# A hybrid convolution and attention layer on one Trainium2 core: first products taken slice by slice, prompt attention in fixed rows, a shorter norm at the end

## The chip, the cores and the metric

The kernel runs on one core of one Trainium2 chip. The metric is the device time of one execution in microseconds (us), as the median of several. The engines of the core are TensorE (PE; its weight loads are listed as PEld), VectorE (DVE), ScalarE (ACT), GpSimd (POOL) and SyncE (SP), which here only issues DMAs. Each engine works through its own instructions in order, and semaphores tie the engines together. Matmul results go to PSUM, everything else lies in SBUF.

## The reference

One layer of a decoder for 256 prompt tokens and 8 x 4 sample tokens, which share the weights. All 288 tokens go through each product together.

```python
z = x @ w_in                                   # h, gate_b, gate_c, q, k, v, g_a, g_b
ya = gate_b * causal_conv3(gate_c * h)          # mixer A
yb = dilated_window_attention(q, k, v)          # mixer B: 3 groups x 4 heads of 128, ALiBi;
                                                # the softmax of a head runs over its 3 groups
mixed = sigmoid(g_a) * (ya @ w_branch_a) + sigmoid(g_b) * (yb @ w_branch_b)
x1 = layernorm(ALPHA * x + mixed @ w_out)
a, b = split(x1 @ w_up)
y = layernorm(ALPHA * x1 + (silu(causal_conv3(a)) * b) @ w_down)
```

D_MODEL is 2048, D_FF 5632. The outputs are y, the new keys and values, and the rows that the convolutions keep. The sample tokens attend to caches of up to 2048 old rows, the prompt tokens to themselves.

## The kernel before

**Layout and products.** Activations are held feature by token: 128 partitions, 16 slices k, 288 tokens. A product is one block of 128 output features: `product` (L174) takes the next prepared weight block and `mms` (L188) issues, for each of its 16 slices, three matmuls of 288 columns: the rounded weight times the rounded activation (L194), the rounded weight times the activation's remainder (L195), the weight's remainder times the rounded activation (L196). So a block of 16 slices is 48 matmuls.

**Weights.** `prepare` (L161) loads one block of 1 MB into one of three buffers `wst`; `half_block` (L134) makes, for each half of it, the rounded part on ACT (`whi`, L137) and the remainder on VectorE (`wlo`, L138). One block is prepared ahead of its product in the program's text. A scheduler then places the instructions of each engine; the program can hold an order with `behind` (L124), which makes one instruction stand after another of its engine without a wait.

**The start.** L213 is a loop of matmuls on a zero tile, to busy TensorE early. Then x is loaded in four pieces (`FIRST`, L221, issued by ACT), and the first two blocks in the same four pieces each (L232, issued by SP). Rounded parts and remainders follow (L234, L235 for weights, `split`, L200 and L201, for x). The first product then runs over all its slices, and after it the second; the scheduler interleaves them where one has to wait.

**Order of the work.** The first 36 products are 12 query blocks, then four heads of six key and value blocks (their copies are at L435 and L445). Then come 48 products for mixer A, the gates, the branches, w_out, and the feed-forward part in three thirds. After a head's keys and values, `prompt_attention` (L271) is written out in full: the values are transposed (L276) and copied out of PSUM; for each half of the queries come three score matmuls (L283), the bias on VectorE (L285), maximum, exponential and scaling (L289 to L293), then for each half of the keys three transposes (L298), a copy (L300) and three value matmuls (L302). All of these use the two PSUM buffers `att`. The scheduler places these matmuls among the products that follow.

**Sample attention.** `sample_steps` (L342) is a generator; `product` takes a step of it from time to time. A step is a visit: 16 or 64 records of small matmuls with 32 rows of output on a cache tile (scores at L356, values at L407), into the PSUM buffer `long`, and the load of the next cache tiles.

**Norms.** `Norm` (L542 on) keeps sums on POOL, squares on ACT, and at the end multiplies by a matrix of ones on TensorE (L572, L573). The reciprocal root is made by Ln (L608 for the last norm), Exp (L609) and one Newton step (L616, L617). Ln and Exp lie in different activation tables, and the table of Ln is called early by a dummy activation (L568). `finish_out` (L593 on) splits the last pass among VectorE and POOL (subtract the mean and multiply by the factor, L604) and ACT and VectorE (gain and shift, L630 and L628), and stores y in six pieces (L631).

Of the kernel before, what the change touches and what calls it, by code (L numbers as in the profile page):

```python
# [17 lines left out]
P = 128  # L18
D = 2048
KD = D // P  # L20
# [45 lines left out]
FIRST = ((0, 2), (2, 6), (8, 4), (12, 4))  # L66

N_WARM = 20
# [14 lines left out]
def layer_kernel(ctx: ExitStack, tc: tile.TileContext, ins, outs):  # L83
# [89 lines left out]

    def product(x):  # L174
# [12 lines left out]

    def mms(out, w, x):  # L188
        nk = sum(n for _, _, n in w)
        k = 0  # L190
        for hi, lo, n in w:
            for c in range(n):
                xh_k, xl_k = (t[:, k].rearrange("p h a -> p a h") for t in x)
                pe.matmul(out, hi[:, c, :], xh_k, start=k == 0, stop=False)  # L194
                pe.matmul(out, hi[:, c, :], xl_k, start=False, stop=False)  # L195
                pe.matmul(out, lo[:, c, :], xh_k, start=False, stop=k == nk - 1)  # L196
                k += 1
# [22 lines left out]
    for k0, n in FIRST:  # L220
        act.dma_start(xs[:, k0 : k0 + n, :], x_in[:, k0 : k0 + n, :])  # L221
    w_ready = []
    stage = []
    for b in range(2):
        stage.append((sb(wp, [P, KD, P], "wst"), ins["w_in"][b].rearrange("p (k c) -> p k c", c=P)))
        halves = [[sb(wp, [P, HK, P], n, F32R, bufs=4) for n in ("whi", "wlo")] + [HK] for _ in range(2)]
        w_ready.append(halves)
    for k0, n in FIRST:
        k = slice(k0, k0 + n)
        h = slice(k0 % HK, k0 % HK + n)  # L230
        for b, (st, src) in enumerate(stage):
            sp.dma_start(st[:, k, :], src[:, k, :])  # L232
            hi, lo, _ = w_ready[b][k0 // HK]
            act.copy(hi[:, h, :], st[:, k, :])  # L234
            dve.tensor_tensor(lo[:, h, :], st[:, k, :], f32(hi[:, h, :]), ALU.subtract)  # L235
            if b == 0:
                split(xh[:, k, :, :H], xl[:, k, :, :H], h3(xs[:, k]))
    x = (xh[:, :, :, :H], xl[:, :, :, :H])
    x_gb = (xh[:, :, :, :HG], xl[:, :, :, :HG])

# [13 lines left out]
    sT_two = [xs_flat[:, c * NG * P : (c + 1) * NG * P].rearrange("p (g q) -> p g q", g=NG) for c in range(2)]  # L254
    oT_two = [xs_flat[:, c * P + 6 * P : c * P + 7 * P] for c in range(2)]
    q_all = xs_flat[:, 8 * P : 8 * P + NH * NG * T].rearrange("p (j g t) -> p j g t", j=NH, g=NG)
# [13 lines left out]

    def prompt_attention(j, qT, kT, vT):  # L271
        v = v_two[j % 2]
        for kb in range(2):
            pv = att(NG * P)
            for g in range(NG):
                pe.transpose(pv[:, g * P : (g + 1) * P], vT[:, g, kb * P : (kb + 1) * P], ident)  # L276
            act.copy(v[:, kb], pv.rearrange("p (g d) -> p g d", g=NG))
        for qb in range(2):
            nk = P * (qb + 1)
            s = s_two[qb][:, : NG * nk].rearrange("p (g k) -> p g k", g=NG)  # L280
            for g in range(NG):
                p = att(nk)
                pe.matmul(p, qT[:, g, qb * P : (qb + 1) * P], kT[:, g, :nk], start=True, stop=True)  # L283
                c0 = qb * NG * P + g * nk
                dve.scalar_tensor_tensor(  # L285
                    s[:, g, :], m_dist[:, c0 : c0 + nk], -SLOPE[g][j] / SCALE, p, ALU.mult, ALU.add
                )
            st = sb(wk, [P, 4], "st", bufs=4)
            dve.reduce_max(st[:, 0:1], s, AX.XY)  # L289
            dve.tensor_scalar_mul(st[:, 1:2], st[:, 0:1], -SCALE)  # L290
            act.activation(s, s, AF.Exp, bias=st[:, 1:2], scale=SCALE, accum_out=st[:, 2:3])
            dve.reciprocal(st[:, 3:4], st[:, 2:3])
            dve.tensor_scalar_mul(s, s, st[:, 3:4])  # L293
            po = att(P)
            for kb in range(qb + 1):
                pt = att(NG * P)
                for g in range(NG):
                    pe.transpose(pt[:, g * P : (g + 1) * P], s[:, g, kb * P : (kb + 1) * P], ident)  # L298
                sT = sT_two[kb]
                act.copy(sT, pt.rearrange("p (g q) -> p g q", g=NG))  # L300
                for g in range(NG):
                    pe.matmul(po, v[:, kb, g, :], sT[:, g, :], start=kb == 0 and g == 0, stop=kb == qb and g == NG - 1)  # L302
            oT = oT_two[qb]
            act.copy(oT, po)
            split(ybh[:, j, qb * P : (qb + 1) * P], ybl[:, j, qb * P : (qb + 1) * P], oT)
# [36 lines left out]
    def sample_steps():  # L342
        fetch_two()
        yield
        s = sw2[:, :SW]
        sbias = cst[:, C_SB : C_SB + SW]
        for g in range(NG):
            qm = by_batch(q_s[:, g])
            cols = P if g == 0 else NT * P
            p = sb(ps, [P, cols], "long", bufs=1)  # L350
            for b in range(NB):
                if g > 0 or b % 4 == 0:
                    c = cache_tiles.pop(0)
                o = (b % 4) * NH * P if g == 0 else 0
                for j in range(NH):
                    pe.matmul(  # L356
                        p[j * NS : (j + 1) * NS], qm[:, j, b, :], c[:, o + j * cols : o + (j + 1) * cols],
                        start=b == 0, stop=b == NB - 1,
                    )
                if b == NB - 1 or (g > 0 and b % 2 == 1):  # L360
                    fetch_two()
# [35 lines left out]
        for g in range(NG):  # L397
# [4 lines left out]
            for b in range(NB):  # L402
# [3 lines left out]
                for j in range(NH):  # L406
                    pe.matmul(  # L407
                        p[j * NS : (j + 1) * NS], sm[:, j, b, :], c[:, o + j * cols : o + (j + 1) * cols],
                        start=b == 0 and g < 2, stop=b == NB - 1 and g == 2,
                    )  # L410
                if b == NB - 1 or (g > 0 and b % 2 == 1):
                    fetch_two()
                    yield
# [18 lines left out]
    kv = sb(big, [P, 2, 2, NG, T], "dd")  # L432
    for j in range(NH):
        for g in range(NG):
            act.copy(h2(q_all[:, j, g]), product(x))  # L435
            if j == 0 and g > 0:
                for dst, src in ((cst, ins["cst"][:, :C_M0]), (m_dist, ins["cst"][:, C_M0:])) if g == 1 else ((prm, ins["prm"]),):
                    behind(sp.dma_start(dst, src), w_load[0])
        pool.tensor_copy(q_s[:, :, j, :], q_all[:, j, :, SEQ:])
    steps_on[0] = True  # L440
    for j in range(NH):
# [8 lines left out]
        prompt_attention(j, q_all[:, j], kT, vT)  # L450
# [43 lines left out]
    yah = sb(big, [P, KD, T], "yah", F32R)  # L494
    yal = sb(big, [P, KD, T], "yal", F32R)
    cm = sb(big, [P, KD, 2 + 2 * NB], "cm")
    for i in range(KD):
# [10 lines left out]
        pb = product(x)  # L508
        ya = sb(wk, [P, T], "ya", bufs=2)
# [32 lines left out]
    class Norm:  # L542
# [13 lines left out]
        def add(self, i):  # L556
# [9 lines left out]
            if i == KD - 2:  # L566

                act.activation(lw[:, 3, 0:1], q[:, 0:1], AF.Ln)  # L568
# [9 lines left out]
        def finish(self):  # L578
# [5 lines left out]
            act.activation(t, v, AF.Ln)  # L584
            act.activation(r, t, AF.Exp, scale=-0.5)
# [7 lines left out]
        def finish_out(self, y, out):  # L593
# [11 lines left out]

            for k0, n in MEAN_POOL:
                by_token(pool, k0, n, mu, ALU.subtract)
            act.activation(t, v, AF.Ln)  # L608
            act.activation(r, t, AF.Exp, scale=-0.5)  # L609
            with tc.issue_after(i_v.ins):  # L610
                for k0, n in MEAN_DVE:
                    i_m = by_token(dve, k0, n, mean, ALU.subtract)

            act.activation(t, r, AF.Square)
            with tc.issue_after(i_m.ins):
                dve.scalar_tensor_tensor(t, t, -0.5, v, ALU.mult, ALU.mult)  # L616
                i_r = dve.scalar_tensor_tensor(dev, t, 1.5, r, ALU.add, ALU.mult)  # L617
            act.copy(r_pool, dev)
            for k0, n in OUT_POOL:
                by_token(pool, k0, n, r_pool, ALU.mult)  # L620
            with tc.issue_after(i_r.ins):
                for k0, n in OUT_DVE:
                    i_m = by_token(dve, k0, n, dev, ALU.mult)
            for k0, n in OUT_ORDER:
                for i in range(k0, k0 + n):
                    if i in OUT_LAST:
                        with tc.issue_after(i_m.ins):
# [271 lines left out]
```

## Time and profile before

| | us |
|---|---|
| median of 3 runs | 1771.77 |
| lowest and highest of them | 1770.14 and 1772.48 |
| profiled execution | 1772.71 |
| its span, first to last instruction | 1770.9 |

| stretch of the profiled execution | from the span's start, us |
|---|---|
| first matmul on the zero tile | 1.22 |
| first product matmul | 5.41 |
| first and last record of prompt attention on TensorE | 119.25, 290.3 |
| first and last visit of sample attention | 146.49, 706.3 |
| last product matmul starts | 1752.47 |
| last output DMA issued, landed | 1766.26, 1769.93 |

A row of the timeline gives the start, the duration, the engine, the line, the operation, what is written and read, the shape and the count; a wait stands in brackets with what ended it. A float32 matmul of the attention shows as two records, a transpose or a product matmul as one. Matmuls overlap in their records, so the pace is read from the distance of their starts.

### The profile page before, as it was taken

Reading aid. Unit: us, or ns where it says so; the run is one execution under the profiler, and the core shown is the slowest. Engines: PE = TensorE matmul, PEld = TensorE weight load, DVE = VectorE, ACT = ScalarE, POOL = GpSimd, SP = SyncE. Lnnn points to the kernel's source line nnn. Section 1 sums busy time; section 2 is a strip of 40 time slices with the busy share of each in tenths; the row PEclk is TensorE's granted clock in tenths of the full one; section 3 lists DMA queues with packets and bytes.
Section 4 is the critical chain, followed back from the end, with each engine's and each line's share of the span. In section 5 each row is a group of like instructions: output and inputs, shape, how many; then the busy total and the mean of one; then the engine's idle time right before and its main releaser. Section 6 shows DMA issues by size and latency. Waiting matters only on the chain.

```text
span 1770.9 us, 33606 instructions
## 1 busy us (share of the span) xinstructions
PE 1749.3 (99%) x14277; PEld 1717.1 (97%) x14277; DVE 1010.0 (57%) x1321; ACT 800.8 (45%) x1178; POOL 252.4 (14%) x402
## 2 busy tenths in 40 slices
PE   8999999999999999999999999999999999999996
PEld 8999899999999999999999999999999999999996
DVE  4445446555645444455688787774555554555564
ACT  5444434333434333344455655553444443345444
POOL 0000000000000000001255233320011110011174
PEclk9999999999999999999999999999999999999998
DMA  8476677788787787467766566666666666666652
GB/s 305 172 301 258 258 292 272 288 304 316 260 322 301 296 322 264 151 247 270 283 218 235 214 226 226 226 226 223 229 227 226 230 222 233 219 236 219 242 191 104
DMA packets 59430, 436.25 MB, mean 246 GB/s; under 512 B 7184, under 2 KB 7696, under 8 KB 15248
## 3 DMA queue, kind: packets, MB, share of 16 engines
q1 hardware_dynamic: 57552, 428.22, 66.1%
q10 hardware_dynamic: 1728, 5.90, 0.9%
q8 instruction: 111, 1.82, 0.4%
q14 instruction: 39, 0.32, 0.0%
HBM read 389.89 MB, written 94.53 MB: 274 GB/s over the span
## 4 chain that ended last, share of the span: by engine, by line
PE 97%; ACT 1%; DVE 1%; DMA 0%; POOL 0%; issue 0%; ACTq 0%; DVEq 0%
PE acc L194 31%; PE acc L196 31%; PE acc L195 31%; PE long L356 1%; PE long L407 1%; DMA yah<-in_x 0%; PE att L283 0%; PE att L302 0%; ACT yah L630 0%; POOL qk_s L478 0%; DVE dd L604 0%; PE att L298 0%; ACT whi L137 0%; ACT xh L200 0%; PE att L276 0%
## 5 line engine op out<-in xcount | busy, mean ns | idle before, releaser
L138 DVE TENSOR_TENSOR wlo<-wst,whi 128x1024 fp32r<-128x1024 f32 (+1 forms) x580 | 710.5, 1225 | 608.0 <-ACT whi L137 602.1
L137 ACT CAST whi<-wst 128x1024 fp32r<-128x1024 f32 (+1 forms) x580 | 592.3, 1022 | 864.3 <-PE acc L195 763.6
L194 PE MATMUL acc<-xh,whi 128*128 128x288 f32 (+1 forms) x3264 | 940.1, 288 | 2.7 <-ACT whi L234 2.7
L196 PE MATMUL acc<-xh,wlo 128*128 128x288 f32 (+1 forms) x3264 | 937.3, 287 | 0.3 <-DVE wlo L235 0.3
L195 PE MATMUL acc<-xl,whi 128*128 128x288 f32 (+1 forms) x3264 | 936.3, 287 | 0.9 <-DVE xl L201 0.9
L194 PEld LDWEIGHTS acc<-xh,whi 128*128 128x128 f32 x3264 | 618.1, 189 | 14.0 <-issue 3.8
L196 PEld LDWEIGHTS acc<-xh,wlo 128*128 128x128 f32 x3264 | 618.1, 189 | 1.7 <-issue 0.8
L195 PEld LDWEIGHTS acc<-xl,whi 128*128 128x128 f32 x3264 | 618.3, 189 | 1.5 <-DVE xl L201 1.1
L194 PE MATMUL acc<-yah,whi 128*128 128x288 f32 x1216 | 348.2, 287 | 0.3 <-ACT yah L200 0.3
L196 PE MATMUL acc<-yah,wlo 128*128 128x288 f32 x1216 | 347.8, 286 | 0.0
L195 PE MATMUL acc<-yal,whi 128*128 128x288 f32 x1216 | 347.6, 286 | 0.0
L194 PEld LDWEIGHTS acc<-yah,whi 128*128 128x128 f32 x1216 | 229.7, 189 | 3.2 <-ACT h L519 2.5
L195 PEld LDWEIGHTS acc<-yal,whi 128*128 128x128 f32 x1216 | 229.8, 189 | 0.1
L196 PEld LDWEIGHTS acc<-yah,wlo 128*128 128x128 f32 x1216 | 229.8, 189 | 0.1
L478 POOL COPY qk_s<-u 128x2 f32<-128x2 f32 x44 | 41.7, 947 | 573.7 <-ACT u L680 441.5
L464 DVE SCALAR_TENSOR_TENSOR cy<-u,prm,cy 128x304 f32<-128x304 f32 x120 | 71.2, 594 | 3.3 <-ACT cy L462 0.6
L534 POOL TENSOR_TENSOR ya<-ya,dd 128x288 f32<-128x288 f32 x16 | 13.6, 849 | 306.0 <-DVE ya L533 306.0
L489 DVE TENSOR_TENSOR ya<-cy,acc 128x144 f32<-128x144 f32 x132 | 25.7, 249 | 33.0 <-PE acc L196 33.0
L478 POOL COPY cm<-u 128x2 f32<-128x2 f32 x16 | 3.0, 185 | 257.2 <-DVE u L505 257.2
L200 ACT CAST yah<-ya 128x288 fp32r<-128x288 f32 x76 | 32.7, 431 | 15.1 <-POOL ya L534 8.4
L201 DVE TENSOR_TENSOR yal<-ya,yah 128x288 fp32r<-128x288 f32 x76 | 34.9, 460 | 1.1 <-ACT yah L200 1.1
L462 ACT ACTIVATE cy<-u,prm 128x304 f32<-128x304 f32 x60 | 32.9, 549 | 3.1
(158 smaller groups left out, 791.8 us busy)
## 6 DMA issues: line engine op xcount, KB each, us to landing
wst<-in_w_in SPq DMA_DIRECT2D x114, 1024.0 KB, 6.1
wst<-in_w_up SPq DMA_DIRECT2D x88, 1024.0 KB, 4.8
wst<-in_w_down SPq DMA_DIRECT2D x32, 1024.0 KB, 4.9
cache<-in_ck SPq DMA_DIRECT2D x18, 1024.0 KB, 6.4
out_o_ck<-cache SPq DMA_DIRECT2D x18, 1024.0 KB, 9.2
cache<-in_cv SPq DMA_DIRECT2D x18, 1024.0 KB, 6.3
out_o_cv<-cache SPq DMA_DIRECT2D x18, 1024.0 KB, 9.9
wst<-in_w_a SPq DMA_DIRECT2D x16, 1024.0 KB, 4.9
```

Of the source, the lines that this page charges most:

```text
L137: act.copy(hi[:, :n, :], st[:, k0 : k0 + n, :])
L138: dve.tensor_tensor(lo[:, :n, :], st[:, k0 : k0 + n, :], f32(hi[:, :n, :]), ALU.subtract)
L194: pe.matmul(out, hi[:, c, :], xh_k, start=k == 0, stop=False)
L195: pe.matmul(out, hi[:, c, :], xl_k, start=False, stop=False)
L196: pe.matmul(out, lo[:, c, :], xh_k, start=False, stop=k == nk - 1)
L200: act.copy(hi, src)
L201: dve.tensor_tensor(lo, src, f32(hi), ALU.subtract)
L356: pe.matmul(p[j * NS : (j + 1) * NS], qm[:, j, b, :], c[:, o + j * cols : o + (j + 1) * cols], start=b == 0, stop=b == NB - 1,)
L462: act.activation(y, u[:, :YW], AF.Copy, scale=prm[:, w0 : w0 + 1])
L464: dve.scalar_tensor_tensor(y, u[:, i : i + YW], prm[:, w0 + i : w0 + i + 1], y, ALU.mult, ALU.add)
L478: pool.tensor_copy(dst[:, 0:2], u[:, SEQ : SEQ + 2])
L489: dve.tensor_tensor(a, b, c, ALU.mult)
```

## The change

1. **Start.** The first two weight blocks are loaded together into a buffer of their own, in six slices instead of four, each beside the same slice of x. `first_two` issues both products interleaved: slice by slice, term by term, block by block, held in this order. The zero loop has 18 matmuls instead of 20. The constants, the distances and the parameters are loaded during the second head's queries, not the first's.
2. **Prompt attention** becomes a generator with three rows: all scores of a head; two products later all transposes (values, then softmax); one product later all value matmuls. `product` takes it forward. Each row is chained behind the last matmul of the product before it. The softmax of both halves lies between rows 1 and 2. One `acc` buffer joins the two `att` buffers in rows 1 and 2.
3. **Sample visits** are chained: the matmuls of one visit stand in the order of the text.
4. **Norms.** The reciprocal root's seed comes from Abs_reciprocal_sqrt instead of Ln and Exp, in both norms. In the last pass, VectorE, POOL and ACT share the slices in another way, and VectorE makes the Newton step after its first subtraction instead of its third.

```diff
-FIRST = ((0, 2), (2, 6), (8, 4), (12, 4))
+FIRST = ((0, 2, "act"), (2, 2, "act"), (4, 2, "act"), (6, 2, "act"), (8, 4, "sp"), (12, 4, "sp"))
-N_WARM = 20
+N_WARM = 18
-MEAN_DVE = ((0, 3), (3, 3), (6, 3))
-MEAN_POOL = ((9, 1), (10, 2), (12, 2), (14, 2))
-OUT_DVE = ((0, 1), (1, 3), (4, 3), (7, 4))
-OUT_POOL = ((11, 1), (12, 2), (14, 2))
-OUT_ORDER = ((0, 1), (1, 3), (4, 3), (7, 4), (11, 3), (14, 2))
-OUT_LAST = (9, 10, 11, 12, 13)
+NORM_DVE = ("m", 0, 3), ("r", 0, 3), ("m", 3, 3), ("r", 3, 3), ("m", 6, 2), ("r", 6, 2), ("r", 8, 2), ("r", 10, 2)
+MEAN_POOL = (8, 2), (10, 2), (12, 2), (14, 2)
+OUT_POOL = (12, 2), (14, 2)
+GB_DVE = (8, 9, 10, 11)
+OUT_ORDER = (0, 3), (3, 3), (6, 2), (8, 4), (12, 2), (14, 2)
...
+    def prompt_step():
+        if prompt[0]:
+            prompt[1] -= 1
+            if prompt[1] <= 0:
+                prompt[1] = next(prompt[0], None)
+                if prompt[1] is None:
+                    prompt[0] = None
...
         o = acc(x[0].shape[-1])
         mms(o, w, x)
+        prompt_step()
...
+    w_two = sb(big, [P, 2, KD, P], "dd")
+    w_two_hi = sb(big, [P, 2, KD, P], "yal", F32R)
+    w_two_lo = [sb(wk, [P, 2, HK, P], "cache", F32R, bufs=2) for _ in range(2)]
+    w_in_two = ins["w_in"][0:2].rearrange("b p (k c) -> p b k c", c=P)
+    for k0, n, queue in FIRST:
+        k = slice(k0, k0 + n)
+        (act if queue == "act" else sp).dma_start(xs[:, k], x_in[:, k])
+        sp.dma_start(w_two[:, :, k], w_in_two[:, :, k])
+    for k0, n, _ in FIRST:
+        k = slice(k0, k0 + n)
+        split(xh[:, k, :, :H], xl[:, k, :, :H], h3(xs[:, k]))
+        split(w_two_hi[:, :, k], w_two_lo[k0 // HK][:, :, k0 % HK : k0 % HK + n], w_two[:, :, k])
+    def first_two():
+        prepare()
+        o = [acc() for _ in range(2)]
+        before = None
+        for k0, n, _ in FIRST:
+            for term in range(3):
+                for k in range(k0, k0 + n):
+                    xk = x[term == 1][:, k].rearrange("p h a -> p a h")
+                    for b in range(2):
+                        w = w_two_lo[k // HK][:, b, k % HK] if term == 2 else w_two_hi[:, b, k]
+                        i = pe.matmul(
+                            o[b], w, xk, start=k == 0 and term == 0, stop=k == KD - 1 and term == 2
+                        )
+                        if before is not None:
+                            behind(i, before)
+                        before = i
+        return [t.rearrange("p a h -> p h a") for t in o]
...
+    def in_a_row(row):
+        for before, i in zip(row, row[1:]):
+            behind(i, before)
+
     def prompt_attention(j, qT, kT, vT):
+        blocks = [(qb, g, P * (qb + 1)) for qb in range(2) for g in range(NG)]
+        s3 = att(NG * P), att(2 * 2 * P), sb(ps, [P, 2 * P], "acc")
+        p_at = [(s3[0], g * P) for g in range(NG)] + [(s3[1], 0), (s3[1], 2 * P), (s3[2], 0)]
+        in_a_row([last_mm[0]] + [
+            pe.matmul(t[:, c : c + nk], qT[:, g, qb * P : (qb + 1) * P], kT[:, g, :nk], start=True, stop=True)
+            for (t, c), (qb, g, nk) in zip(p_at, blocks)
+        ])
...
+        yield 2
         v = v_two[j % 2]
+        pv = [att(NG * P) for _ in range(2)]
+        row = [last_mm[0]] + [
+            pe.transpose(pv[kb][:, g * P : (g + 1) * P], vT[:, g, kb * P : (kb + 1) * P], ident)
+            for kb in range(2) for g in range(NG)
+        ]
         for kb in range(2):
...
+            act.copy(v[:, kb], pv[kb].rearrange("p (g d) -> p g d", g=NG))
+        pairs = ((0, 0), (1, 0), (1, 1))
+        pt = [att(NG * P), att(NG * P), sb(ps, [P, NG * P], "acc")]
+        in_a_row(row + [
+            pe.transpose(t[:, g * P : (g + 1) * P], s[qb][:, g, kb * P : (kb + 1) * P], ident)
+            for t, (qb, kb) in zip(pt, pairs) for g in range(NG)
+        ])
+        for sT, t in zip(sT_three, pt):
+            act.copy(sT, t.rearrange("p (g q) -> p g q", g=NG))
+        yield 1
+        po = att(2 * P)
+        in_a_row([last_mm[0]] + [
+            pe.matmul(
+                po[:, qb * P : (qb + 1) * P], v[:, kb, g], sT[:, g],
+                start=kb == 0 and g == 0, stop=kb == qb and g == NG - 1,
+            )
+            for sT, (qb, kb) in zip(sT_three, pairs) for g in range(NG)
+        ])
...
                 for j in range(NH):
-                    pe.matmul(
+                    row.append(pe.matmul(
...
                 if b == NB - 1 or (g > 0 and b % 2 == 1):
+                    in_a_row(row)
+                    row = []
...
-            act.copy(h2(q_all[:, j, g]), product(x))
-            if j == 0 and g > 0:
+            act.copy(h2(q_all[:, j, g]), q_first.pop(0) if q_first else product(x))
+            if j == 1:
...
-        prompt_attention(j, q_all[:, j], kT, vT)
+        prompt[:] = [prompt_attention(j, q_all[:, j], kT, vT), 0]
+        prompt_step()
...
-            act.activation(t, v, AF.Ln)
-            act.activation(r, t, AF.Exp, scale=-0.5)
+            act.activation(r, v, AF.Abs_reciprocal_sqrt)
...
+            before = i_v
+            for n_op, (what, k0, n) in enumerate(NORM_DVE):
+                with tc.issue_after(before.ins):
+                    before = by_token(dve, k0, n, *((mean, ALU.subtract) if what == "m" else (dev, ALU.mult)))
+                if n_op == 0:
+                    with tc.issue_after(before.ins):
+                        dve.scalar_tensor_tensor(t, t, -0.5, v, ALU.mult, ALU.mult)
+                        before = dve.scalar_tensor_tensor(dev, t, 1.5, r, ALU.add, ALU.mult)
+                    act.copy(r_pool, dev)
```

In the program as built, a visit of the sample attention stands inside row 2 of every head, between the transposes of the values and those of the softmax, and all other rows and visits stand between two products or, for the middle of the sample attention, within one.

More of the change, by code (lines that the diff above doesn't have):

```diff
@@ L195, in mms @@
                 pe.matmul(out, hi[:, c, :], xl_k, start=False, stop=False)
-                pe.matmul(out, lo[:, c, :], xh_k, start=False, stop=k == nk - 1)
+                last_mm[0] = pe.matmul(out, lo[:, c, :], xh_k, start=False, stop=k == nk - 1)
                 k += 1
@@ L269, in layer_kernel @@
     v_s = sb(big, [P, NH, NG, NS], "v_s")
+    def in_a_row(row):
+        for before, i in zip(row, row[1:]):
+            behind(i, before)
     def prompt_attention(j, qT, kT, vT):
-        v = v_two[j % 2]
-        for kb in range(2):
[L274 to L305, printed above, removed]
@@ new lines, in prompt_attention @@
+        for (t, c), (qb, g, nk) in zip(p_at, blocks):
+            c0 = qb * NG * P + g * nk
+            dve.scalar_tensor_tensor(
+                s[qb][:, g, :], m_dist[:, c0 : c0 + nk], -SLOPE[g][j] / SCALE, t[:, c : c + nk], ALU.mult, ALU.add
+            )
+        for qb in range(2):
+            st = sb(wk, [P, 4], "st", bufs=4)
+            dve.reduce_max(st[:, 0:1], s[qb], AX.XY)
+            dve.tensor_scalar_mul(st[:, 1:2], st[:, 0:1], -SCALE)
+            act.activation(s[qb], s[qb], AF.Exp, bias=st[:, 1:2], scale=SCALE, accum_out=st[:, 2:3])
+            dve.reciprocal(st[:, 3:4], st[:, 2:3])
+            dve.tensor_scalar_mul(s[qb], s[qb], st[:, 3:4])
@@ L508, in layer_kernel @@
         pb = product(x)
+        if i == 0:
+            yah, yal = (sb(big, [P, KD, T], n, F32R) for n in ("yah", "yal"))
         ya = sb(wk, [P, T], "ya", bufs=2)
@@ L566, in add @@
             if i == KD - 2:
[L568 removed]
+                act.activation(lw[:, 3, 0:1], q[:, 0:1], AF.Abs_reciprocal_sqrt)
             if last:
```

64 lines of the change are left out of this document (23 added, 41 removed).

## The prediction

> **What bounds the kernel now.** I read the page first, then the waits, the start, one visit of the sample attention, and the tail.
>
> ```profile
> span 1770.9 us, 33606 instructions
> PE 1749.3 (99%) x14277; PEld 1717.1 (97%) x14277; DVE 1010.0 (57%) x1321; ACT 800.8 (45%) x1178; POOL 252.4 (14%) x402
> ...
> PE 97%; ACT 1%; DVE 1%; DMA 0%; POOL 0%; issue 0%; ACTq 0%; DVEq 0%
> ```
>
> TensorE is busy from end to end, and the chain that ended last is 97% TensorE. So time can come from three places only: the start before TensorE runs at its pace, work on TensorE that is not product, and the tail after the last product. The waits of TensorE, complete but for a first 1.2 us on its own zero tile, all lie in the start:
>
> ```profile
> PE acc L194 <- ACT whi L234: 2.7, 2, 1.7
> ...
> PE acc L195 <- DVE xl L201: 0.9, 1, 0.9
> PE acc L194 <- ACT yah L200: 0.3, 1, 0.3
> PE acc L196 <- DVE wlo L235: 0.3, 1, 0.3
> ```
>
> The start has a second loss that no wait shows. In the timeline, product matmuls are 0.24 us apart from 12.52 to 18.04, and 0.1225 us apart afterwards:
>
> ```profile
> 12.52 0.45 PE L194 MATMUL acc<-xh,whi 128*128 128x288 f32 x1
> ...
> 12.76 0.45 PE L195 MATMUL acc<-xl,whi 128*128 128x288 f32 x1
> ...
> 18.18 0.29 PE L194 MATMUL acc<-xh,whi 128*128 128x288 f32 x1
> ...
> 18.31 0.29 PE L195 MATMUL acc<-xl,whi 128*128 128x288 f32 x1
> ```
>
> The windows of the same stretches show why: the granted clock is 1.00, then 0.50 (the last three figures are PEclk, the DMA engines' share and GB/s).
>
> ```profile
> 4.42:11.25 6.83, 3.29 (x23) 2.66 (x21) 3.63 (x5) 4.75 (x6) 0.00 (x0) 1.00 1.01 410
> 11.25:18.08 6.83, 6.57 (x26) 6.25 (x27) 6.62 (x8) 4.25 (x7) 0.00 (x0) 0.50 1.03 398
> ```
>
> TensorE was busy for 3.29 of 6.83 us (48%) and was then given half the clock for the next 6.83 us. The same rows show the DMA engines full at about 410 GB/s.
>
> **The start.** The edit loads the first two weight blocks together, slice by slice beside x, and runs both products interleaved, so that every slice that lands feeds 6 matmuls per k.
> Before: counted in the timeline, 39 product matmuls have started by 18.04; the other 57 of the first two blocks' 96 take 57 x 0.1225 = 7.0, so both end at 25.2.
> After: x is 2.36 MB, two blocks are 2.10 MB. Windows of 2 us show 8 and 200 GB/s up to 4.0 us, that is 0.42 MB, then about 410 GB/s. The remaining 4.04 MB take 9.85 us; with 0.25 for the completion the last slice is there at 14.1. Its cast (1024 columns, as L137: 1.05) ends at 15.15, and its 24 matmuls end at 15.15 + 2.9 = 18.1; their remainders (L138: 1.23, done 16.4) are needed only from 17.1. Earlier slices: the first lands near 4.9, two casts (0.67 and 0.57) bring the first matmul to about 5.9, and 96 x 0.1225 = 11.8 gives 17.7 as the floor. Allowing for a queue at ACT, where a weight cast that is waiting for its slice stands ahead of an x cast, I take 18.5 (to 19.0). Then block 3: 1.05 MB behind the others lands at 16.7, its first cast ends 17.8, its first remainder 19.0, and its third matmul needs that; it effectively starts at 18.75. Gain 25.2 - 18.75 = 6.4. Bounds: 7.0 with no queue and no wait; 3.5 if the clock halves (below) and slices are late as well. Constants, distances and parameters (cst, m_dist, prm: three DMAs on SP's queue) now stand behind block 4 in place of block 2; attention, their first reader, begins at 119 us before, so this costs nothing and takes 1.6 MB out of the way of blocks 3 and 4.
>
> A page of the Trainium skill, "TensorE: Matmul & The Clock Gate" (Part 1), says that the clock halves after an idle window of about 3.4 us; here it halved with no idle stretch longer than 1.65 us, so the trace differs, and I go by the busy share of the window. By the page's rule the changed start would not go cold either.
>
> **TensorE's attention work.** The instructions stay the same: per head 15 transposes at 0.109 us, 6 score matmuls (0.222 for 128 keys, 0.43 for 256) and 9 value matmuls (0.223). Does a scattered piece cost more than a long row? A lone score matmul, products on both sides, takes 0.222 us off the product stream; six value-matmul records in a row take 0.67, 0.111 each; four transposes 0.44, two 0.22. So the price is per instruction and rows save nothing there. It differs for the sample visits, whose 32-row matmuls run four at a time:
>
> ```profile
> 219.54 1.92 PE L356 MATMUL long<-cache,sw 128*32 128x512 f32 x16
> ...
> 255.94 1.06 PE L356 MATMUL long<-cache,sw 128*32 128x512 f32 x8
> 256.94 0.49 PE L283 MATMUL att<-dd,yah 128*128 128x128 f32 x2
> 257.36 1.04 PE L356 MATMUL long<-cache,sw 128*32 128x512 f32 x2
> 258.33 0.49 PE L283 MATMUL att<-dd,yah 128*128 128x128 f32 x2
> 258.75 1.06 PE L356 MATMUL long<-cache,sw 128*32 128x512 f32 x6
> ```
>
> The whole visit takes 2.05 us off the products (219.32, the product before it, to 221.62, the second after it, less two intervals). The one cut in three takes 4.00 (255.73 to 259.97, less two intervals); less 2.05 and two scores at 0.222, the two cuts cost 1.50. Another visit, cut in two at 181.63, costs 1.17 by the same sum. The change chains each visit, and in the order of the changed kernel's TensorE instructions only the first one (of 128 columns) is still cut, at about 0.3. Term: -(1.50 + 1.17) + 0.3 = -2.4; from -2.7 to 0.
>
> **What the fixed places can cost.** Row 1 (scores) stands right after a head's last key and value products, row 2 (transposes of values, then of the softmax) two products later, row 3 (values times softmax) one product after that. All products stand behind a row that waits. Row 2 has two inputs.
> (a) The softmax. VectorE needs, from L285, L289, L290, L292, L293: 2.1 + 1.5 + 0.3 + 0.3 + 1.0 = 5.3, and four weight remainders at 1.22 stand among them: 10.2. There are two products (48 x 0.1225 = 5.9 each), six transposes (0.65) and, in the built order, a sample visit (2.0) inside row 2: 14.4. Cover 4.2.
> (b) The transposed values share two PSUM buffers with the transposed softmax, so two ACT copies (L300's shape, 0.48 each) stand between them. From the third transpose to the first that needs the buffer are 0.3 + 2.0 = 2.3 us, thanks to that visit; ACT needs at worst a cast (1.05), a product's copy (0.42) and the copy itself: 1.95. Cover about 0.3. One more cast ahead of it would cost 0.7 in each head, 3 in all; without the visit, up to 1.6 in each. I take +0.4, with bounds 0 and +3.
> Rows 1 and 3 wait for copies that have a whole product (5.9) to be done.
>
> **The tail.** The norm's seed takes one instruction in place of Ln, a table load and Exp:
>
> ```profile
> 1755.74 1.28 ACT L609 ACT_TABLE_LOAD   x1
> 1757.03 0.41 ACT L609 ACTIVATE acc<-cache 128x288 f32<-128x288 f32 x1
> ```
>
> VectorE's factor is ready after the seed (1755.31 + 0.41), Square (0.41), and two operations of 0.45 to 0.48 that now stand behind one subtraction instead of three: 1757.15 instead of 1759.02. That is not what is saved, as ends are set by POOL and ACT. POOL has twelve blocks as before (0.68 each, from 1755.03): its last product comes at 1763.2. ACT, 0.52 a step, has twelve outputs in place of eleven: three from 1758.2, three from 1760.2, two by 1762.9, then the POOL ones, 1763.9 and 1765.0; before it ended at 1766.23. The last output's issue, and 3.7 us from issue to landing, follow. Term -1.25; from 0 (POOL and DVE slow each other more) to -1.9 (the whole lead).
> A page of the Trainium skill, "ScalarE: Activation LUTs" (What ACT_TABLE_LOAD costs), puts a switch at 1.28 us plus a drain of 1.38. The trace shows 1.28 and the next activation 0.01 us later, so no drain; by the page the sum below would be up to 1.4 larger.
> The first norm, near 975 us, lies under products on both sides: nothing.
>
> **Sum.** -6.4 - 2.4 + 0.4 - 1.25 = -9.65 us. The profiled execution took 1772.71 (its span 1770.9 and 1.8 around it); the median shown is 0.9 below it. Forecast: 1771.77 - 9.65 = 1762.1 for the median.
>
> **Rivals.**
> 1. Cold start. If the changed start leaves TensorE under about half busy in a window, it gets half the clock as before. With the window of 11.25 to 18.08 and 48 matmuls done at 12.4, 23 more by 18.08 and 25 after, the pair ends at 21.1, 2.4 later than forecast: 1764.5. For it: 1 KB pieces in the first slices (128 partitions x 2 blocks), four small slices at only 1.4 us each for 1.5 us of matmuls. Against it: by the landings above TensorE is busy about two thirds of the first window and more later. 16%.
> 2. The rows pay for themselves. ACT's cast order costs row 2 its 3 us and the visits inside rows keep their cuts' price: -6.4 + 0.6 - 1.25 = -7: 1764.7. For: the cover is 0.3 only. 9%.
> 3. Slower: the softmax comes late. In the trace of before, the last score of the first half (129.42) to its transposes (135.64) is 6.2, and of the second half 143.75 to 151.54 is 7.8; put end to end, 14.0 against the 14.4 there are. From 14.4 on each us costs four, one in each head. To be slower by 0.2% it must be 3.3 us late: -9.65 + 13.2 = +3.5: 1775.3. Against: those 7.8 include the pieces' own places in the order. 5%.
> 4. Nothing moves: the first loads come no faster, or the gain of the start is lost since blocks come too late afterwards, leaving the visits and the tail and losing them to (b): 1770.5. Against: a block takes 2.6 us of DMA and 5.9 of TensorE. 5%.
> The forecast holds 65%.
>
> **How the numbers follow.** Within 0.2% (3.5 us, about what a measurement of this kernel can tell) lie rival 4 and edges: 5%. Slower 5%, faster 90%. The range takes 7.0 + 2.7 + 1.9 for the low end, 1760.2, and rivals 1 and 2 with part of their bounds for the high one: -4.9, 1766.9.
>
> **What would show it.** The 96th product matmul near 18.5 instead of 25.2, no half clock between 4.4 and 40 us; no L407 visit of 16 records cut; TensorE waits before L340 under 0.5 us a head; one table load in the tail, and ACT's last output 1.2 us sooner after the last product. Wrong would make it: a PEclk of 0.5 near 15 us, waits at L340 for ACT's copies or VectorE's scaling, or a wait for block 3 over 1 us.

## The result and the profile after

| | before | after |
|---|---|---|
| median, us | 1771.58 (6 runs) | 1764.34 (6 runs) |
| lowest and highest | 1770.14, 1772.48 | 1764.20, 1764.45 |
| profiled execution | 1772.71 | 1764.45 |
| its span | 1770.9 | 1762.7 |

The ratio is 0.996, with a 95% interval from 0.9948 to 0.9972: 7.2 us faster, where 9.65 were forecast. The runs of after lie within 0.25 us of each other, those of before within 2.3.

The page of after, parts 1 and 4:

```profile
span 1762.7 us, 33587 instructions
PE 1744.4 (99%) x14275; PEld 1713.7 (97%) x14275; DVE 1008.0 (57%) x1317; ACT 797.3 (45%) x1167; POOL 254.1 (14%) x401
...
PE 97%; DMA 1%; ACT 1%; DVE 1%; POOL 0%; issue 0%; SPq 0%; ACTq 0%; DVEq 0%
```

TensorE bounds it as before. Its waits in the profile of after:

```profile
PE acc L227 <- DVE cy L224: 1.2, 1, 1.2
PE acc L262 <- ACT yal L214: 1.2, 2, 0.7
PE acc L208 <- ACT yah L214: 0.3, 1, 0.3
PE acc L262 <- ACT xh L214: 0.2, 1, 0.2
```

L262 is the interleaved pair of first blocks; no wait stands at the transposes or at any row of the prompt. The windows of the start show a full clock (the last three figures are PEclk, the DMA engines' share and GB/s):

```profile
4.42:11.25 6.83, 5.79 (x37) 4.83 (x36) 4.46 (x7) 4.64 (x8) 0.00 (x0) 1.00 1.03 379
11.25:18.08 6.83, 6.41 (x52) 6.19 (x51) 5.91 (x6) 4.52 (x5) 0.00 (x0) 1.00 1.05 419
```

TensorE was busy for 5.79 of the first 6.83 us, where it had been busy for 3.29. The price is in the last column: 379 GB/s instead of 410.

Since products follow each other without a wait after the start, three numbers from each trace hold the whole span: when the first two blocks' 96 product matmuls are done (the start of the 99th, less two intervals of 0.1225), the stretch from there to the last product matmul, and the tail after it. Where the 99th has to wait for block 3, as in after, that wait counts with the start: there the 97th stands at 20.05 already.

| profile | first two blocks done | to the last product | tail | half clock in the start | median, us |
|---|---|---|---|---|---|
| before | 25.17 | 1727.3 | 18.5 | 6.83 | 1771.58 |
| after | 20.34 | 1725.0 | 17.3 | 0 | 1764.34 |
| start alone | 19.92 | 1727.4 | 18.4 | 0 | 1767.57 |
| rows alone | 22.32 | 1724.9 | 18.5 | 0 | 1769.13 |
| visits' chain alone | 23.89 | 1727.3 | 18.5 | 3.41 | 1771.70 |
| norms alone | 23.85 | 1727.3 | 17.3 | 3.41 | 1770.84 |
| before, 40 zero matmuls | 22.28 | 1727.3 | 18.5 | 0 | 1770.03 |
| after, weights by 4 slices | 20.60 | 1724.9 | 17.2 | 0 | 1764.58 |
| after, visits out of row 2 | 19.92 | 1729.7 | 17.3 | 0 | 1768.68 |
| after, slices of 4 | 22.79 | 1724.9 | 17.4 | 3.41 | 1766.66 |
| after, once more | 19.92 | 1725.0 | 17.3 | 0 | 1763.97 |
| after, block 3 cast in quarters | 19.48 | 1724.9 | 17.3 | 0 | 1763.78 |

The span of the profiled before and after differs by 4.83 + 2.3 + 1.1 = 8.2 us, the medians by 7.2. The difference of 1.0 is that of the two profiled runs: before's lies 1.1 over its median, after's 0.1 over its own, and the sections below find before's part in the start. After's start varies too: three more profiles with it (start alone, visits out of row 2, once more) have 19.92.

### The profile page after: what moved, and what is told of

Its sections match the earlier page's. It is cut to its first block, busy times and chain, and to the rows that moved or that the text cites. A ratio compares the mean times of both kernels' runs of the same rounds, so it can differ in the third digit from the quotient of the medians.

```text
span 1762.7 us, 33587 instructions
## 1 busy us (share of the span) xinstructions
PE 1744.4 (99%) x14275; PEld 1713.7 (97%) x14275; DVE 1008.0 (57%) x1317; ACT 797.3 (45%) x1167; POOL 254.1 (14%) x401
## 4 chain that ended last, share of the span: by engine, by line
PE 97%; DMA 1%; ACT 1%; DVE 1%; POOL 0%; issue 0%; SPq 0%; ACTq 0%; DVEq 0%
PE acc L208 31%; PE acc L209 31%; PE acc L210 31%; PE long L407 1%; PE long L460 1%; DMA wst<-in_w_in 1%; PE att L348 0%; DMA dd<-in_w_in 0%; PE att L312 0%; ACT whi L138 0%; POOL qk_s L535 0%; ACT yah L685 0%; DVE dd L661 0%; ACT xh L214 0%; PE att L340 0%; PE att L332 0%
## 5 line engine op out<-in xcount | busy, mean ns | idle before, releaser
L208 PE MATMUL acc<-xh,whi 128*128 128x288 f32 (+1 forms) x3232 | 928.0, 287 | 0.0
L210 PE MATMUL acc<-xh,wlo 128*128 128x288 f32 (+1 forms) x3232 | 925.4, 286 | 0.1
L209 PE MATMUL acc<-xl,whi 128*128 128x288 f32 (+1 forms) x3232 | 925.0, 286 | 0.0
L208 PEld LDWEIGHTS acc<-xh,whi 128*128 128x128 f32 x3232 | 610.8, 189 | 8.0 <-ACT cy L519 2.5
L210 PEld LDWEIGHTS acc<-xh,wlo 128*128 128x128 f32 x3232 | 610.8, 189 | 1.2 <-issue 0.8
L209 PEld LDWEIGHTS acc<-xl,whi 128*128 128x128 f32 x3232 | 610.9, 189 | 0.4 <-issue 0.2
L622 POOL TENSOR_TENSOR cache<-cache,dd 128x288 f32<-128x288 f32 x28 | 27.7, 988 | 46.6 <-DVE dd L701 31.5
```

The lines of the kernel that those rows point to most:

```text
L210: last_mm[0] = pe.matmul(out, lo[:, c, :], xh_k, start=False, stop=k == nk - 1)
L622: pool.tensor_tensor(self.s1, self.s1, d, ALU.add)
```

## The experiments

### Each part of the change alone

Four kernels, each the kernel before with one part. Together the four parts are the change, but for the place where two buffers are allocated. The start alone:

```diff
-FIRST = ((0, 2), (2, 6), (8, 4), (12, 4))
-N_WARM = 20
+FIRST = ((0, 2, "act"), (2, 2, "act"), (4, 2, "act"), (6, 2, "act"), (8, 4, "sp"), (12, 4, "sp"))
+N_WARM = 18
...
+    q_first = first_two()
```

> The kernel before with the new start alone (two blocks by slices of x, 18 zero matmuls, constants later). Theory: the start is one part that adds to the others; between the profiles of before and after it is worth 25.17 - 20.34 = 4.8 us, so the time is 4 to 5 us under before, the third block's third matmul stands near 20.6, and no half clock is granted. It also sets the spread: 2.3 us between the runs of before, under 0.4 us here. Rival: part of the start's gain belongs to the rest of the change (blocks later in the order); then under 3 us, or over 6.

Measured: 1767.57 (1767.38 to 1767.79, 11 runs) against 1771.59 (1769.73 to 1772.99, 33 runs of before on the same chip): ratio 0.9977 (0.9968 to 0.9986), 4.0 us. The third block's third matmul stands at 20.16, the clock is full, and the spread is 0.4 us. So the start is a part by itself, and the narrow spread comes with it. The 4.0 us lie at the lower end of the 4 to 5 that were expected from the two profiles.

The prompt's rows alone (`prompt_attention` as a generator, `prompt_step` in `product`, the layout of its buffers):

> The kernel before with prompt attention in three rows alone; sample visits are not chained. Theory: it is the rows that keep the visits whole, since no score or value matmul of the prompt is loose any more that could be set between a visit's matmuls: -2.0 to -2.5 us, the visits of 16 records whole, no wait at the transposes. Rival: the chaining of the visits keeps them whole; then within 0.5 us of before.

Measured: 1769.13 (1767.47 to 1770.46), ratio 0.9987 (0.9978 to 0.9995), 2.5 us. The middle stretch is 1724.9 instead of 1727.3: 2.4 us, which is the whole of after's gain there. In this trace, without any chain, the four visits of 16 records are whole (they start at 174.29, 217.18, 253.55 and 262.13), where two of before's four are cut.

The visits' chain alone:

```diff
-                    pe.matmul(
+                    row.append(pe.matmul(
...
+                    in_a_row(row)
+                    row = []
```

> The kernel before with the sample visits chained alone. Theory: the chain holds an order among a visit's matmuls but lets others stand between them, so visits are still cut in two or three: within 0.6 us of before. Rival: the chain makes the visits whole: -2.3 us.

Measured: 1771.70 (1771.08 to 1772.87), ratio 1.0003 (0.9994 to 1.0012): nothing. A visit in its timeline (start, duration, what, count):

```profile
180.35 1.06 PE L362 MATMUL long<-cache,sw 128*32 128x512 f32 x6
181.34 0.94 PE L307 MATMUL att<-yah,yal 128*128 128x128 f32 x6
182.11 0.60 PE L288 MATMUL att<-dd,yah 128*128 128x256 f32 x2
182.64 1.90 PE L362 MATMUL long<-cache,sw 128*32 128x512 f32 x10
```

The 16 records of the visit are in their order, and value and score matmuls stand between the sixth and the seventh all the same. An order among a visit's own matmuls keeps nothing else out. In after the same stretch of work reads:

```profile
171.66 0.82 PE L332 MATMUL att<-cst,dd 128*128 128x128 f32 x6
172.40 1.92 PE L407 MATMUL long<-cache,sw 128*32 128x512 f32 x16
174.26 0.87 PE L340 MATMUL att<-cst,yal 128*128 128x128 f32 x6
174.97 0.49 PE L340 MATMUL acc<-cst,yal 128*128 128x128 f32 x3
```

The visit is whole since the prompt's matmuls are tied to rows of their own, and it stands inside row 2.

The norms alone (Abs_reciprocal_sqrt, the new shares of the last pass):

> The kernel before with the new norms alone. Theory: only the tail of the last norm moves, by 18.43 - 17.36 = 1.07 us between the profiles: -0.9 to -1.3 us, nothing near the first norm. Rival: the reciprocal root's lead of 1.9 us is saved whole (-1.9), or the tail's gain came from the shifted DMA order and is 0.

Measured: 1770.84 (1768.65 to 1772.09), ratio 0.9996 (0.9987 to 1.0005). The interval takes in no change, since the old start's spread is wider than the effect; the trace is clearer: the tail is 17.3 instead of 18.5, close to that of every kernel with the new norms (17.2 to 17.4), and the middle is 1727.3, so the first norm moved nothing.

The four medians' differences add up to -4.0 - 2.5 + 0.1 - 0.75 = -7.15; the change measured -7.2. That they meet so closely is partly luck, since the norms' -0.75 is not clear of zero and their trace says -1.1.

### What halves the clock in the old start

The three profiles above that keep the old start do not agree about it: the first two blocks were done at 22.3, 23.9 and 23.9, and in the profile of before at 25.2. The clock was halved for 0, 3.41, 3.41 and 6.83 us. Cut at the moments where the granted clock changes, and at half their distance, the stretches of 3.41 us read as below, for before, and then for the rows alone. With the rows alone no change falls into the start, so the cuts are counted back from one in the tail: in before the changes at 11.25 and in the tail at 1758.87 lie 512 steps of 3.4133 us apart, and 510 such steps before the rows' change at 1751.56 is 10.76.

```profile
4.42:7.83 3.41, 2.39 (x19) 2.18 (x18) 1.61 (x3) 1.50 (x4) 0.00 (x0) 1.00 1.00 408
7.83:11.25 3.42, 0.90 (x7) 0.48 (x5) 2.02 (x2) 3.25 (x3) 0.00 (x0) 1.00 1.03 412
```

```profile
4.00:7.35 3.35, 2.81 (x12) 2.46 (x12) 1.39 (x3) 1.38 (x3) 0.00 (x0) 1.00 1.03 406
7.35:10.76 3.41, 1.90 (x12) 1.48 (x12) 1.69 (x2) 3.12 (x3) 0.00 (x0) 1.00 1.02 414
10.76:14.18 3.42, 2.40 (x17) 2.19 (x18) 3.42 (x5) 2.93 (x5) 0.00 (x0) 1.00 1.06 399
```

In before, a stretch in which TensorE was busy for 0.90 of 3.42 us came just ahead of the half clock. With the rows alone the start's program was the same, but the stretches lay 0.5 us earlier (10.76 for 11.25), the poorest after 4 us held 1.90 us, and no half clock followed. With the chain alone and the norms alone, the stretch ahead of the half clock held 0.72 and 0.78 us. So by these four profiles it is the run's phase against the idle stretch that decides. One caution on PEclk: no record covers the time ahead of 4.42 in before and of 7.35 with the rows alone, and a PEclk of 1.00 says nothing there; the matmuls ahead of it are 0.24 us apart, the pace of the half clock. To test the idle stretch, it was filled:

```diff
-N_WARM = 20
+N_WARM = 40
```

> The kernel before with 40 matmuls on the zero tile instead of 20. In the profiles with the old start the clock was halved for 6.83, 3.41, 3.41 and 0 us, and the first two blocks ended at 25.2, 23.9, 23.9 and 22.3 us. Theory: the half clock comes from a window in which TensorE was busy for too little of the time, and which window that is varies from run to run; 20 more zero matmuls fill the first idle stretch, so no half clock: the blocks end near 22.4 in every run, the time is 1.5 to 2.5 us under before and its spread falls from 3 us to under 1. Rival: the half clock has another cause, or the zero matmuls delay the product: time as before or up to 2 us over, with the same spread.

Measured: 1770.03 (1769.81 to 1770.96, 11 runs), ratio 0.9991 (0.9982 to 1.0), 1.6 us under before, spread 1.15 (1.92 for the runs of before on the same chip), where under 1 was expected. The first two blocks were done at 22.28, and the stretch is full (here no record covers the time ahead of 7.30, and the zero matmuls up to there are 0.24 us apart):

```profile
4.42:11.25 6.83, 6.67 (x42) 6.45 (x40) 3.61 (x5) 4.91 (x6) 0.00 (x0) 1.00 1.03 417
11.25:18.08 6.83, 6.34 (x49) 6.14 (x50) 6.64 (x8) 4.65 (x7) 0.00 (x0) 1.00 1.04 405
```

So the half clock follows the idle stretch, and a kernel with the old start pays for it by chance: none, 1.6 or 2.9 us in the four profiles (23.9 or 25.2 against 22.3). Of the new start's 4.0 us, then, about 1.6 are the half clock's, which 20 more zero matmuls take away as well, and about 2.4 are the slices' (19.92 against 22.3). Why the half clock lasted 6.83 us in before and 3.41 in the others stays open: TensorE was busy for 3.15 us of its first 3.41 in before, and for 2.94 with the chain alone, where the full clock came back.

### Why the new start was 1.6 us later than worked out

The last slice landed at 15.71, not at 14.1, and the slices before it were late as well. The first theory was the piece size: 1 KB runs of weights.

```diff
-        sp.dma_start(w_two[:, :, k], w_in_two[:, :, k])
+        if k0 % 4 == 0:
+            sp.dma_start(w_two[:, :, k0 : k0 + 4], w_in_two[:, :, k0 : k0 + 4])
```

with the casts of x and weights chained in the order of the slices.

> The changed kernel with the weights of the first two blocks in pieces of 4 slices (2 KB runs) instead of 2 (1 KB runs) for the first half, x as it was, and the casts of x and weights held in the order of the slices. Theory: the runs of 1 KB beside x held the DMA engines to 341 and 367 GB/s between 4 and 8 us, where they gave 418 and 415 before, and so the last slice landed at 15.7 and not at 14.1: here it lands near 14.3, the blocks end at 18.8 to 19.3, block 3's third matmul comes at 19.1 to 19.5 instead of 20.6: 0.7 to 1.3 us under the changed kernel's 1764.3. Rival: the rate was low for another cause in the first 8 us; then the last slice lands near 15.7 again and the time is within 0.3 us of 1764.3.

Measured: 1764.58 (1764.49 to 1764.74): no gain. From 4 to 8 us the DMA engines gave 354 GB/s, as in after (354), though no run was under 2 KB; the last slice landed at 15.23. The start's 1 KB runs gave 379 and 388 GB/s, and a last landing at 15.29 and 15.30, in the profiles of the start alone and of after once more. So 1 KB runs are not shown to be the cause, and the theory falls. x's third slice landed at 9.90 instead of 8.89, behind the larger pieces beside it, and TensorE waited 1.2 us at one slice.

A second try took away the small pieces altogether:

```diff
+FIRST = ((0, 4, "act"), (4, 4, "act"), (8, 4, "act"), (12, 4, "act"))
```

> The changed kernel with x and the first two blocks in four equal slices of 4 instead of 2, 2, 2, 2, 4, 4. Theory: all pieces are 2 KB or more, so the last slice lands at 14.3 to 14.6 and not 15.7, but the first product matmul starts at 7.6 to 8.2 instead of 6.3, and TensorE, which needs 11.8 us for the two blocks, ends them at 19.8 to 20.3: within 0.6 us of the changed kernel's 1764.3 either way. Rival: the end of the two blocks is set by the last landing; then they end at 14.5 + 1.1 + 2.9 = 18.5 and the time falls by 1.2 us or more. The idle stretch of 2.5 us before the first product can also cost the clock; then it is 2 us or more over.

Measured: 1766.66 (1766.34 to 1767.09), 2.3 us over after. The rate was 387 GB/s between 4 and 8 us, but the last slice landed at 15.44 all the same, the first product matmul waited until 8.44, and the clock was halved:

```profile
5.18:8.59 3.41, 0.62 (x5) 0.38 (x4) 1.23 (x2) 2.10 (x2) 0.00 (x0) 1.00 1.02 378
8.59:12.01 3.42, 3.42 (x15) 3.42 (x16) 1.27 (x1) 1.04 (x2) 0.00 (x0) 0.50 1.01 391
```

This is a cold start as in the prediction's first rival, at 0.62 us of work in 3.41: the first two blocks were done at 22.8, 2.45 later than in after. The half clock's share of that is not separated, since the first product matmul also came 2.2 us later.

What the trace of after shows of the 1.6 us is this. The slice that TensorE last waited for is the fifth, not the last: its weights landed at 12.94, their cast ended at 14.02, and from 14.06 on TensorE took the remaining 48 matmuls without a wait, so that the pair ended at 20.05; the last slice's cast was done at 16.78, 0.3 us before its first matmul. By the working's own rate the fifth slice would have been there at 11.4 (12 of 16 slices are 3.34 MB). Three things make up the 1.5 us between. By 12.4 us, when its last packets moved, 3.65 MB had gone, where the working had 3.86: 0.5 us. Of the 3.65, 0.3 MB were the last slice's x, issued later and served beside it: 0.7 us. And the landing was told about 0.5 us after the last packets, where the working took 0.25, a term that no run shows: 0.3 us. Block 3's load was served in the same way: its first packets, of 8 KB, moved at 14.19, and the last packet of the slices ended at 15.18. This part is read from packets, and no run took it away.

The profile of before could have warned of it. It loads the same 4.46 MB for x and two blocks, and there the last piece landed at 15.46. Block 3's first cast began at 18.06 in before, in after at 18.23, where the working had 16.75:

```profile
18.06 1.05 ACT L137 CAST whi<-wst 128x1024 fp32r<-128x1024 f32 x1 [1.96 <-DMA wst<-in_w_in]
```

So the new start brought no load earlier at its end. What it gained came from more matmuls on each slice as it landed (TensorE was busy for 5.79 us between 4.42 and 11.25 instead of 3.29), and from the clock.

### What covers the wait in row 2

```diff
-        in_a_row(row + [
+        row_two[0] = in_a_row(row + [
...
-                    in_a_row(row)
+                    in_a_row(([row_two[0]] if row_two[0] else []) + row)
```

where `in_a_row` returns the last of its row.

> The changed kernel with each sample visit held behind the row of transposes before it, so that no visit stands inside that row. Theory: inside the row the visit covers the two copies out of PSUM that the row waits for; without it TensorE waits about 1.0 to 1.6 us in each of four heads: 4 to 6.5 us over the changed kernel's 1764.3, waits at the softmax's transposes for ACT's copies of the values. Rival: the copies are done in time without it, or the visit costs as much inside the row as it covers: within 1 us of 1764.3.

Measured: 1768.68 (1768.57 to 1769.16), 4.3 us over after, with four waits of 3.9 in all. One of them:

```profile
172.12 0.82 PE L335 MATMUL att<-cst,dd 128*128 128x128 f32 x6
173.98 0.93 PE L343 MATMUL att<-cst,yal 128*128 128x128 f32 x6 [1.04 <-ACT yal L339]
```

In after a visit of 1.9 us stands at this place, and there is no wait. Without the visit there, the row would have taken back 4.3 of the 7.2 us. The change's text does not ask for the visit there; the scheduler set it.

### A little more

The start's next bound is block 3: in after its third matmul waits for the remainder of its first half.

```diff
+        step = n // 2 if loads[0] == 1 else n
+        for c in range(0, n, step):
...
+            act.copy(hi[:, c : c + step, :], st[:, k, :])
+            dve.tensor_tensor(lo[:, c : c + step, :], st[:, k, :], f32(hi[:, c : c + step, :]), ALU.subtract)
```

> The changed kernel once more, unchanged, beside the next one on the same chip. The parts measured alone add up to -4.0 (start) - 2.5 (rows) + 0.1 (chain) - 0.75 (norm) = -7.15 us; theory: they are independent, so 1764.2 to 1764.6 again, with a spread under 0.5.

> The changed kernel with block 3's casts and remainders in quarters instead of halves. In the changed kernel block 3's third matmul stands at 20.58, 0.29 us later than TensorE's pace from the second would have it, and waits for the remainder of the first half. Theory: a quarter is ready 0.5 + 0.6 us sooner, so that wait goes: 0.2 to 0.4 us under the changed kernel beside it. Rival: smaller casts cost ACT and VectorE fixed time and the wait moves to a later quarter: within 0.1 us.

Measured: the changed kernel 1763.97 (1763.86 to 1764.42), with quarters 1763.78 (1763.49 to 1763.83), 5 runs each. The changed kernel's second and third matmul of block 3, and then those with quarters:

```profile
19.80 0.29 PE L209 MATMUL acc<-xl,whi 128*128 128x288 f32 x1
20.17 0.39 PE L210 MATMUL acc<-xh,wlo 128*128 128x288 f32 x1
```

```profile
19.60 0.29 PE L212 MATMUL acc<-xl,whi 128*128 128x288 f32 x1
19.73 0.29 PE L213 MATMUL acc<-xh,wlo 128*128 128x288 f32 x1
```

The changed kernel came out 0.2 under the 1764.2 to 1764.6 that were expected, and its spread was 0.56 where under 0.5 was. The wait of 0.25 is gone, and the medians differ by 0.19, just under the 0.2 to 0.4 expected. This is the fastest of the kernels here, by less than the runs' own spread of 0.3 to 0.6; that it is faster is likely, since its slowest run (1763.83) is under the other's fastest (1763.86), but it is small.

## Why the prediction was right, and by how much it missed

**The bound.** TensorE end to end: right. Start, middle and tail move separately, and the parts measured alone add up to the whole within what the runs can tell.

**The start** was forecast at -6.4; this is the step that was mis-sized. It measured -4.83 between the two profiles and -4.0 between medians. Two things were left out.
First, the slices were taken to land in the order of their issue at 410 GB/s: last slice 14.1, block 3 at 16.7. They landed at 15.71 and 18.2, about where the same bytes had landed in before. TensorE had the work's pace as forecast, and the first matmul came at 6.26 for 5.9, but it waited for slices in between, last for the fifth:

```profile
14.06 1.25 PE L262 MATMUL acc<-xh,yal 128*128 128x288 f32 x8 [0.42 <-ACT yal L214]
...
18.23 2.00 ACT L138 CAST whi<-wst 128x1024 fp32r<-128x1024 f32 x2 [1.45 <-DMA wst<-in_w_in]
...
20.58 0.39 PE L210 MATMUL acc<-xh,wlo 128*128 128x288 f32 x1
```

The 99th product matmul at 20.58 waits for block 3's remainder, as the working had it, 1.6 us later than it had it (1.2 in three more profiles of this start). That wait is worth 0.3 us; the rest had come with the slices. The constants changed nothing for block 3: they were issued behind it in before too (at 10.00, block 3 at 9.08), and behind block 5 in after.
Second, the profile of before was a draw with the longest half clock (6.83 us); the profiled run lies 1.1 over the median of the six. The working took this one start as the start of the kernel, carried its whole difference to the median, and so counted as gain 1.1 us that the median run of before does not lose.

**The clock.** That the changed start stays warm was right. The rival's price, 2.4, is close to the 2.45 between after and the slices of 4, but by luck: it was worked out for a half clock of 6.83 us, and there it lasted 3.41, after a first product 2.2 us later. The unit, half of 6.83 us, was wrong: in the slices of 4 TensorE was busy for 4.03 of the 6.82 us up to 8.59 (59%) and got the half clock all the same. In the three profiles whose windows are shown, stretches of 3.41 us with 0.90 and 0.62 us of work were followed by half clock and one with 1.90 was not; where between them the limit lies is not measured. The rule of the Trainium skill's page "TensorE: Matmul & The Clock Gate" (Part 1) has the window right, about 3.4 us; that it needs to be idle does not agree with the trace, where a quarter of busy time (0.90 of 3.42 us) was not enough.

**The visits** were forecast at -2.4 and measured -2.3 to -2.4: right in size. The cause named was wrong: it was put to the chaining, which alone measured 0.1; the rows did it.

**Row 2** was given +0.4 with bounds 0 and 3: no wait was measured. That the visit inside the row covers the two copies was right; without it the wait, given as up to 1.6 in each head, measured 1.0.

**The tail**, -1.25: -1.1 in the traces, but the size is partly luck. The factor was ready at 1750.00, 2.3 us after the variance's operation began (L657, 1747.68), where it had taken 4.2 (1754.81 to 1759.02): as worked out. ACT's last output, however, ended 13.04 us after the last product matmul's start, against 13.76 in before: 0.7 sooner, not 1.2. The working let VectorE multiply as soon as the factor was there; in both traces it first waits 0.46 or 0.47 us for ACT's copy of the factor. The missing 0.4 came behind the last output, which landed 3.25 us after its issue instead of 3.67; why is not shown. That POOL would set the ends beside ACT was not borne out: it takes 8.2 us for its six instructions, but the chain that ended last runs over VectorE and ACT, and ACT's last nine outputs follow each other without a wait. Before's last ACT outputs, and then rows of after:

```profile
1760.94 5.29 ACT L630 ACTIVATE yah<-dd,prm 128x288 f32<-128x288 f32 x10 [0.34 <-DVE dd L604]
```

```profile
1747.89 8.21 POOL L661 TENSOR_TENSOR dd<-dd,cache 128x576 f32<-128x576 f32 x6 [4.41 <-ACT cache L656]
...
1749.54 0.46 DVE L675 SCALAR_TENSOR_TENSOR long<-cache,acc 128x288 f32<-128x288 f32 x1
...
1750.47 1.05 DVE L661 TENSOR_TENSOR dd<-dd,long 128x864 f32<-128x864 f32 x1 [0.47 <-ACT cache L676]
...
1753.61 4.77 ACT L685 ACTIVATE yah<-dd,prm 128x288 f32<-128x288 f32 x9 [0.39 <-DVE dd L661]
```

**The rivals.** The softmax was never late, the gain did not leak away, and rows paid nothing. None of them happened; the miss of 2.4 us is the start's: 1.6 from the landings and about 0.8 to 1.1 from the draw, less small gains elsewhere.

## What to carry to other kernels

Before you cost an edit at a place where the clock or a queue depends on chance, compare the profiled execution with the spread of the runs: if the spread is wider than the term, the profile is one draw, and the term is worth what the median run loses by it. When you work out when loads land, look first where the same bytes landed in the trace you have. Chaining a group of instructions keeps their order and keeps nothing out; to keep a group whole, tie down what could come between. And when a row of dependent work has to wait for evacuations, look for what the scheduler has put into it: here one visit of 1.9 us, which nobody asked for, was worth 4.3 us.

## What the runs showed of the hardware that was not expected

The granted clock changes at steps of 3.41 us whose phase differs from run to run (in profiles of the old start, the half clock began at 11.25, 11.81 and 11.98, or not at all). In four profiles a stretch with 18 to 26% of work (0.62 to 0.90 us) was followed by half clock; one with 56% (1.90 us) was not. DMA loads issued one after another on a queue are not served strictly in that order: in after block 3's packets moved from 14.19 on, while the last packet of the slices ahead of it ended at 15.18.
